# Fourteen projection blocks by seven quarter products, and four pooling gates beside the scan

## Chip, cores, metric

The kernel runs on one core of one Trainium2 chip. The metric is the device time of one execution in microseconds, median of the runs.

## What is computed

One layer of a decoder trunk, all in float32, for x of 1024 tokens by 1024 channels. An RMS norm makes h; one input projection of h (1024 by 13856) is cut into pieces for three branches; each branch is projected back, the three are mixed by sigmoid gates, projected once more, added to x and normed.

```python
h = rms_norm(x, norm_w)
proj = h @ w_in
z, xbc, dt_raw, pool_u, pool_gate, qkv, sb_gate, merge = split(proj)
y_ssm  = mamba2_branch(z, xbc, dt_raw, ...) @ w_proj_ssm    # causal conv of width 4 and SiLU on xbc, then a chunked scan
y_pool = pool_branch(pool_u, pool_gate, ...) @ w_proj_pool  # (trailing means - u) @ pool_w * scale * silu(pool_gate)
y_sb   = stick_breaking_branch(qkv, sb_gate) @ w_proj_sb    # attention with products of (1 - sigmoid), times silu(sb_gate)
g = sigmoid(merge)
merged = g[0] * y_ssm + g[1] * y_pool + g[2] * y_sb
return rms_norm(x + merged @ w_out, final_norm_w)
```

## The kernel before

**Matmuls.** h stands transposed in SBUF, as eight tiles `hT` of 128 channels by 1024 tokens, each as a high part and a low part that together make up the float32 value. The weights are taken in blocks of 256 columns, split in the same way; a product is the three matmuls high-high, high-low, low-high. A block by `gemm_b` is 2 column tiles x 2 token halves x 8 channel tiles x 3 = 96 matmuls of 512 columns (L148). `gemm_a` has the tokens on the other side, 8 token tiles x 24 matmuls of 256 columns (L157), 288 for z0, which takes the 32 dt columns along.

**Weights.** `block_plan` is the list of the 54 input blocks, then those of the output projections. `split_half` takes half a block from a load buffer (two of them): ScalarE casts the high part (L128), VectorE subtracts for the low part (L129), and the next half's load is issued on SP. `block` sees that the halves of its block are split; `mm` hands out PSUM tiles and one split on the way.

**Phases.** First the convolution phase (`conv_part`), where a hand-written order holds for TensorE, VectorE, ScalarE and GpSimd: blocks x0, x1, z0, x2 to x9 (one step of the dt computation, `dt_part`, behind each x block), then g0 to g2, the attention gates. An x block's quarter is read from PSUM by ScalarE (L442) and by three taps on VectorE (L447), then sigmoid (L450), a product on GpSimd (L451) and a store to `d_x`. Three PSUM buffers are added there to the two that all phases share.

Then attention: eight windows, one per pair of heads; in each, matmuls of blocks (v, z, q, k of the next pair, and an `extra` block from `att_fill`) are laid between the attention's own as filling, by a budget in time. Per head and query block: scores (L601, L602), ScalarE (L605, L608), a scan and a product on VectorE (L610, L611), transposes (L628), and the product with v (L651), which waits for VectorE's copy-out `o` (L657). The last window has two filling blocks, m2 and m3.

Then the scan (`ssd_part`) with the eight blocks m4 to m11 as filling, by `merge_gen`, which copies a block to `d_gate`. Then the pool phase (`pool_part`): in turn a u block with the trailing means on VectorE (`mixed`, L728 to L737, up to four adds per column tile for the last group) and a gate block pg with six small matmuls `pp` per quarter (`gated`, L755). Behind it the output projections; their operands x0, x1, ... are loaded from memory and split by `load_x` (L978, L979), the first three of them while the pool phase runs.

## Time and profile before

| | |
|---|---|
| Median of 3 runs | 2082.42 us (2081.85 to 2083.22) |
| Profiled execution | 2080.79 us |
| Its span | 2079.0 us |
| TensorE busy (matmul) | 2048.6 us, 99% |
| VectorE, ScalarE, GpSimd busy | 1203.2, 904.6, 348.9 us |
| Share of the chain that ended last | TensorE 92%, VectorE 4%, ScalarE 2% |

The span is what the profile's rows cover; the profiled execution's own time has 1.8 us around it. A busy time is the sum over an engine's instructions; the chain is the work that ended last, followed back from the end.

### The profile page before, as it was taken

How to read it: one execution, taken by the hardware profiler on the slowest of the kernel's cores; microseconds unless marked ns; L12 is line 12 of the kernel's file. 1: busy time of each engine (PE TensorE's matmuls, PEld its weight loads, DVE VectorE, ACT ScalarE, POOL GpSimd, SP SyncE). 2: the span in 40 equal slices, each digit the busy share in tenths (PEclk: the TensorE clock that was granted, in tenths of full speed). 3: DMA queues.
4: the chain of work that ended last, by engine and by line, in shares of the span. 5: the costliest groups of instructions: out<-in, count | busy, mean ns of one | idle time of the engine just before them, and what ended most of it. 6: DMA issues, size and time to landing. Idle time of an engine off the chain costs nothing.

```text
span 2079.0 us, 29567 instructions
## 1 busy us (share of the span) xinstructions
PE 2048.6 (99%) x11480; PEld 1751.9 (84%) x11480; DVE 1203.2 (58%) x1635; ACT 904.6 (44%) x1841; POOL 348.9 (17%) x415
## 2 busy tenths in 40 slices
PE   8999999999999999999999999999999999999998
PEld 6988889979899998888877877788888888888898
DVE  6466632676666776766774777773545424425333
ACT  5243322555555555555555666763322323323131
POOL 3112200021111111111112344430000002221000
PEclk9999999999999999999999999999999999999999
DMA  4323232112121212212215566654222625433232
GB/s 155 110 94 104 101 104 92 44 54 75 48 72 47 67 57 62 72 41 79 59 51 172 187 203 198 208 163 146 86 76 78 218 96 189 149 101 109 81 133 82
DMA packets 111677, 221.49 MB, mean 107 GB/s; under 512 B 9393, under 2 KB 59313, under 8 KB 111537
## 3 DMA queue, kind: packets, MB, share of 16 engines
q1 hardware_dynamic: 111536, 219.60, 32.4%
q8 instruction: 91, 1.49, 0.3%
q14 instruction: 50, 0.40, 0.1%
HBM read 162.15 MB, written 57.41 MB: 106 GB/s over the span
## 4 chain that ended last, share of the span: by engine, by line
PE 92%; DVE 4%; ACT 2%; issue 1%; DMA 1%; POOL 0%; SPq 0%; DVEq 0%; POOLq 0%; ACTq 0%
PE mm L148 34%; PE mmx L148 24%; PE mm L157 13%; PE mmx L157 4%; PE av L651 3%; PE yd L874 3%; PE tr L628 2%; DVE om L610 2%; PE z L601 1%; PE z L602 1%; PE yo L877 1%; PE st L880 1%; PE pp L755 1%; DVE be L611 1%; PE xp L858 1%
## 5 line engine op out<-in xcount | busy, mean ns | idle before, releaser
L148 PE MATMUL mm<-hT,w 128*128 128x512 f32 x2808 | 717.7, 401 | 3.1 <-DVE hT L345 2.8
L148 PEld LDWEIGHTS mm<-hT,w 128*128 128x128 f32 x2808 | 510.8, 188 | 115.6 <-issue 15.3
L129 DVE TENSOR_TENSOR w<-raw,w 128x1024 fp32r<-128x1024 f32 x142 | 207.7, 1463 | 149.6 <-ACT w L128 149.3
L157 PE MATMUL mm<-w,hT 128*128 128x256 f32 x2112 | 283.9, 286 | 1.2 <-ACT qb L545 1.2
L148 PE MATMUL mmx<-hT,w 128*128 128x512 f32 x1224 | 281.5, 389 | 0.0
L148 PEld LDWEIGHTS mmx<-hT,w 128*128 128x128 f32 x1224 | 229.7, 188 | 47.7
L157 PEld LDWEIGHTS mm<-w,hT 128*128 128x128 f32 x2112 | 263.4, 191 | 2.2 <-ACT qb L545 1.7
L148 PE MATMUL mmx<-x,w 128*128 128x512 f32 x1008 | 230.9, 389 | 0.0
L148 PEld LDWEIGHTS mmx<-x,w 128*128 128x128 f32 x1008 | 189.2, 188 | 39.3
L610 DVE TENSOR_TENSOR_SCAN om<-om,zero 128x128 f32<-128x128 f32 (+7 forms) x128 | 174.4, 1363 | 69.6 <-ACT om L605 69.0
L128 ACT CAST w<-raw 128x1024 fp32r<-128x1024 f32 x142 | 148.6, 1049 | 65.8 <-PE mmx L148 32.3
L630 ACT CAST attT<-tr 128x512 fp32r<-128x512 f32 (+2 forms) x224 | 98.4, 439 | 147.0 <-PE tr L628 79.3
L631 DVE TENSOR_TENSOR attT<-tr,attT 128x512 fp32r<-128x512 f32 (+2 forms) x224 | 111.0, 496 | 76.1 <-ACT attT L630 74.1
L605 ACT ACTIVATE om<-z 128x128 f32<-128x128 f32 (+2 forms) x192 | 92.8, 495 | 78.3 <-PE z L604 75.7
L148 PE MATMUL mm<-x,w 128*128 128x512 f32 x528 | 122.5, 390 | 0.0
L148 PEld LDWEIGHTS mm<-x,w 128*128 128x128 f32 x528 | 98.8, 188 | 21.5 <-ACT x L978 0.7
L1002 ACT ACTIVATE gt<-gt 128x1024 f32<-128x1024 f32 x32 | 34.0, 1062 | 184.0 <-DMA gt<-d_gate 181.3
L851 POOL TENSOR_TENSOR E<-E,cbm 128x1024 f32<-128x1024 f32 x32 | 76.3, 2385 | 161.4 <-issue 121.9
L611 DVE TENSOR_TENSOR be<-be,om 128x128 f32<-128x128 f32 (+7 forms) x128 | 96.9, 757 | 10.4
L1011 POOL TENSOR_TENSOR acc<-acc,gt 128x512 f32<-128x512 f32 x32 | 45.9, 1435 | 293.0 <-DVE gt L1010 293.0
L608 ACT ACTIVATE be<-z 128x128 f32<-128x128 f32 (+2 forms) x192 | 93.0, 498 | 0.1
L628 PE MATMUL tr<-cm,be 128*128 128x128 f32 x576 | 89.5, 273 | 0.5 <-DVE be L611 0.5
(194 smaller groups left out, 2515.6 us busy)
## 6 DMA issues: line engine op xcount, KB each, us to landing
raw<-in_wblk SPq DMA_DIRECT2D x148, 512.0 KB, 3.9
E<-d_act SPq DMA_DIRECT2D x32, 512.0 KB, 4.3
gt<-d_gate SPq DMA_DIRECT2D x32, 512.0 KB, 3.8
d_gate<-mg SPq DMA_DIRECT2D x24, 512.0 KB, 3.4
d_x<-csg SPq DMA_DIRECT2D x16, 512.0 KB, 2.7
xi<-d_x SPq DMA_DIRECT2D x32, 256.0 KB, 3.2
zs<-d_z SPq DMA_DIRECT2D x32, 256.0 KB, 2.8
d_ssm<-yt SPq DMA_DIRECT2D x32, 256.0 KB, 3.1
```

The costliest lines, as they stand in the source:

```text
L128: nc.scalar.copy(hi, raw)
L129: nc.vector.tensor_tensor(out=lo, in0=raw, in1=hi.bitcast(F32), op=ALU.subtract)
L148: T.matmul(ps, w(a, k, ct * P, ct * P + P), mov(b, k, half * 512, half * 512 + 512), start=n == 0, stop=n == 23)
L157: T.matmul(ps, sta(a, k, tok * P, tok * P + P), w(b, k, 0, ncol), start=n == 0, stop=n == 23)
L605: A.activation(om[:, c0 : c0 + n], z[:, 0:n], AF.Sigmoid, scale=-0.125)
L608: A.activation(be[:, c0 : c0 + n], z[:, 0:n], AF.Sigmoid, scale=0.125)
L610: V.tensor_tensor_scan(out=rev, data0=rev, data1=self.zero.broadcast_to((P, L)), initial=1.0, op0=ALU.mult, op1=ALU.add)
L611: V.tensor_tensor(out=be[:, 0:L], in0=be[:, 0:L], in1=om[:, 1 : L + 1], op=ALU.mult)
L628: T.transpose(tr[:, c : c + P], b[:, (2 * jc + j) * P : (2 * jc + j + 1) * P], self.ident)
L630: A.copy(at[:, 0, sl], tr[:, sl])
L631: V.tensor_tensor(out=at[:, 1, sl], in0=tr[:, sl], in1=at[:, 0, sl].bitcast(F32), op=ALU.subtract)
L851: G.tensor_tensor(out=E, in0=E, in1=cbm[:, hg // 2].unsqueeze(1).broadcast_to((P, 8, P)), op=ALU.mult)
```

## The change

Fourteen blocks of the first phase (`SEVEN`: x2 to x9, g2, g3, m4 to m7) are computed by Strassen's scheme in its form with seven products and fifteen sums. A block's weights and h are cut in quarters: weights by channel half and column tile (a11, a12, a21, a22), h by channel half and token half. A product of two quarters is 4 channel tiles x 3 = 12 matmuls of 512 columns.

On h's side four sums of quarters are made once, on VectorE during g0 and g1 (`seven_operands`), split in high and low part by `t_split`, and kept; one of them (t1) takes the place of the upper token half of four hT tiles, which is parked in memory and loaded back behind the last of the blocks (`seven_last`). On the weights' side each block makes four sums (`seven_prep`), in six pieces that stand between the products of the block before. On the output side VectorE makes five adds and ScalarE two copies per block (`seven_block`); six PSUM buffers are added in this stretch. The convolution, gates and stores of a block follow in pieces between the products of the next (`seven_x`, `seven_g`, `seven_m`): an x block now has six taps and two products of 1024 columns on VectorE, and none on GpSimd.

The order in front is now x0, z0, g0, x1, g1 as ordinary blocks. The dt steps stand behind the quarters of x1, where they stood behind whole blocks. Attention's filling has one block less, in the last window only z3. m4 to m7 go to the first phase; the scan's filling is m8 to m11 and the four pg blocks, stored to `d_pg`. In the pool phase `gated` loads the gates from there, in place of a block's matmuls. Smaller: six v buffers for four, two constants made on the chip or loaded later, a smaller DMA scratch.

The diff, cut to its core:

```diff
-    extra = [("g", 3)] + [("z", i) for i in range(1, 4)] + [("m", i) for i in range(4)]
+    extra = [("z", 1), ("m", 0), ("z", 2), ("m", 1), ("m", 2), ("m", 3), ("z", 3)]
...
+SEVEN = [("x", 2), ("m", 4), ("x", 3), ("g", 2), ("x", 4), ("m", 5), ("x", 5), ("m", 6), ("x", 6), ("g", 3), ("x", 7), ("m", 7), ("x", 8), ("x", 9)]
+SCAN_FILL = [(kind, i) for i in range(4) for kind in ("m", "pg")]
+SCAN_FILL = [(kind, i + 8 if kind == "m" else i) for kind, i in SCAN_FILL]
...
-    for i in range(10):
-        part(("x", i), OFF_X + 256 * i)
-        if i == 1:
-            part(("z", 0), OFF_Z + 1024)
-    for i in range(3):
-        part(("g", i), OFF_SG + 256 * i)
+    for kind, i in [("x", 0), ("z", 0), ("g", 0), ("x", 1), ("g", 1)]:
+        part((kind, i), {"x": OFF_X, "g": OFF_SG, "z": OFF_Z + 1024}[kind] + 256 * i)
+    for kind, i in SEVEN:
+        part((kind, i), {"x": OFF_X, "g": OFF_SG, "m": OFF_M}[kind] + 256 * i)
...
-    for i in range(4, 12):
-        merge(i)
-    for g in range(5):
-        if g < 4:
-            part(("u", g), OFF_U + 256 * g)
-        if g > 0:
-            part(("pg", g - 1), OFF_PG + 256 * (g - 1))
+    for kind, i in SCAN_FILL:
+        part((kind, i), {"m": OFF_M, "pg": OFF_PG}[kind] + 256 * i)
+    for g in range(4):
+        part(("u", g), OFF_U + 256 * g)
...
+        def hi(t, c0, c1, src):
+            A.copy(t[:, 0, :, c0:c1], src)
+        def lo(t, c0, c1, src):
+            V.tensor_tensor(out=t[:, 1, :, c0:c1], in0=src, in1=t[:, 0, :, c0:c1].bitcast(F32), op=ALU.subtract)
+        def first():
+            V.tensor_tensor(out=s1, in0=a21, in1=a22, op=ALU.add)
+            V.tensor_tensor(out=s2, in0=s1, in1=a11, op=ALU.subtract)
+        def second():
+            V.tensor_tensor(out=s3, in0=a11, in1=a21, op=ALU.subtract)
+            V.tensor_tensor(out=s4, in0=a12, in1=s2, op=ALU.subtract)
+            hi(t0, 0, P, a11)
+            hi(t2, 0, 256, r1)
+        def third():
+            lo(t0, 0, P, a11)
+            lo(t2, 0, 256, r1)
+            self.load_half()
+            self.load_half()
+        def fourth():
+            hi(t0, P, 256, s2)
+            hi(t1, 0, P, s3)
+        def fifth():
+            lo(t0, P, 256, s2)
+        def sixth():
+            lo(t1, 0, P, s3)
+            hi(t1, P, 256, s1)
+            lo(t1, P, 256, s1)
+            hi(t2, 256, 384, s4)
+            lo(t2, 256, 384, s4)
+        return {1: first, 2: second, 3: third, 4: fourth, 5: fifth, 6: sixth}
...
+        for k in range(4):
+            a, c = self.hT[k], self.hT[4 + k]
+            nc.sync.dma_start(out=self.park[:, k], in_=a[:, :, hi].bitcast(F32))
+            t1 = pool.tile([P, 512], F32, name=f"t1_{k}")
+            d, e = tmp("td"), tmp("te")
+            V.tensor_tensor(out=d, in0=f(a, 0, hi), in1=f(a, 0, lo), op=ALU.subtract)
+            V.tensor_tensor(out=t1, in0=f(a, 1, hi), in1=f(a, 1, lo), op=ALU.subtract)
+            V.tensor_tensor(out=t1, in0=t1, in1=d, op=ALU.add)
+            self.t1.append(t1)
+            V.tensor_tensor(out=e, in0=f(c, 0, hi), in1=t1, op=ALU.subtract)
+            V.tensor_tensor(out=e, in0=e, in1=f(c, 1, hi), op=ALU.add)
+            self.t_split(2, k, e)
+            yield
...
+    def t_split(self, i, k, src):
+        hi, lo = self.tt[i][:, 0, k], self.tt[i][:, 1, k]
+        self.nc.scalar.copy(hi, src)
+        self.nc.vector.tensor_tensor(out=lo, in0=src, in1=hi.bitcast(F32), op=ALU.subtract)
...
+        def product(ps, a, b, first):
+            n = 0
+            for k in range(4):
+                for i, j in ((0, 0), (0, 1), (1, 0)):
+                    T.matmul(ps, w[a](i, k), mov[b](j, k), start=first and n == 0, stop=n == 11, skip_group_check=not first)
+                    n += 1
...
+        x = self.mm()
+        product(x, "a11", "b11", True)
+        A.copy(p1, x)
+        step(0)
+        y = self.mm()
+        product(y, "s2", "t2", True)
+        add(u2, y, p1)
+        step(1)
+        z = self.mm()
+        product(z, "s3", "t3", True)
+        add(u3, z, u2)
+        step(2)
+        v = self.mm()
+        product(v, "s1", "t1", True)
+        add(q(1, 1), v, u3)
+        step(3)
+        product(x, "a12", "b21", False)
+        A.copy(q(0, 0), x)
+        step(4)
+        product(z, "a22", "t4", False)
+        add(q(1, 0), z, u2)
+        step(5)
+        product(v, "s4", "b22", False)
+        add(q(0, 1), v, u2)
+        step(6)
+        return c
...
+        def conv(ct):
+            col = 2 * b + ct
+            nc.gpsimd.memset(c[ct][:, 0:3], 0.0)
+            acc = accs[ct] = self.c_pool.tile([P, S], F32, tag="csg", name="acc", bufs=2)
+            cw = lambda k: self.conv_w[:, col, k : k + 1]
+            nc.scalar.activation(acc, c[ct][:, 3 : 3 + S], AF.Identity, scale=cw(3), bias=self.conv_b[:, col : col + 1])
+            for k in range(3):
+                nc.vector.scalar_tensor_tensor(acc, c[ct][:, k : k + S], cw(k), acc, op0=ALU.mult, op1=ALU.add)
+        def gate(ct):
+            nc.scalar.activation(c[ct][:, 0:S], accs[ct], AF.Sigmoid)
+        def out(ct):
+            col = 2 * b + ct
+            dst = self.d_x[col // 4][:, col % 4] if col < 16 else self.d_bc[:, col - 16]
+            self.silu(c[ct][:, 0:S], accs[ct], c[ct][:, 0:S], dst)
+        return {0: [lambda: conv(0), lambda: gate(0)], 1: [lambda: out(0)], 3: [lambda: conv(1)], 4: [lambda: gate(1)], 5: [lambda: out(1)]}
...
-            nctx = ExitStack()
+            dctx, zctx, nctx = ExitStack(), ExitStack(), ExitStack()
+            dpool = self.sb(dctx, "dt_sb", 1)
+            self.zd = self.sb(zctx, "zd_sb", 1).tile([P, 2, 8, 288], F32R, name="zd")
             norm = self.norm_in(self.sb(nctx, "n_sb", 3), pps)
             for _ in range(3):
                 next(norm)
+            self.drain(self.conv_gen(0, pool, norm))
+            nctx.close()
+            self.zd_open(dpool)
             dt = self.dt_part(dpool)
-            for b in range(10):
-                self.drain(self.conv_gen(b, pool, norm if b == 0 else None))
-                if b == 0:
-                    nctx.close()
-                    self.zd_open(ctx, dpool)
-                else:
+            next(dt)
+            zctx.close()
+            tpool = self.sb(ctx, "t_sb", 1, "right")
+            self.s32pool = self.sb(ctx, "s32_sb", 1, "right")
+            sums = self.seven_operands(tpool)
+            for i, _ in enumerate(self.g_gen(0)):
+                if i % 24 == 12:
+                    next(sums, None)
+            for i, _ in enumerate(self.conv_gen(1, pool)):
+                if i != 3:
                     next(dt, None)
-            for b in range(3):
-                self.drain(self.g_gen(b))
+            self.drain(dt)
+            dctx.close()
+            self.wspool = self.sb(ctx, "ws_sb", 2)
+            self.wseven = {}
+            for i, _ in enumerate(self.g_gen(1)):
+                if i % 18 == 9 and i < 80:
+                    next(sums, None)
+            self.drain(sums)
+            prep = self.seven_prep(BLK[SEVEN[0]])
+            for i in sorted(prep):
+                prep[i]()
+            self.seven_first()
+            plain.close()
+            self.ps_extra(ctx, "seven_ps", 6)
+            make = {"x": self.seven_x, "g": self.seven_g, "m": self.seven_m}
+            before = {}
+            for i, (kind, b) in enumerate(SEVEN):
+                prep = self.seven_prep(BLK[SEVEN[i + 1]]) if i + 1 < len(SEVEN) else {1: self.split_half, 2: self.split_half}
+                before = make[kind](b, self.seven_block((kind, b), before, prep))
+            for i in sorted(before):
+                for f in before[i]:
+                    f()
+            self.seven_last()
...
-                w = self.block(("pg", g))
                 for ct in range(2):
+                    pg = pool.tile([P, S], F32, tag="pgr", name="pgr")
+                    nc.sync.dma_start(out=pg, in_=self.d_pg[:, 2 * g + ct])
                     for half in range(2):
                         hs = slice(half * 512, half * 512 + 512)
-                        ps = self.mm()
-                        self.drain(self.gemm_b(ps, w, ct, self.h, half))
                         sg = pool.tile([P, 512], F32, tag="psg", name="psg")
-                        A.activation(sg, ps, AF.Sigmoid)
-                        V.tensor_tensor(out=sg, in0=sg, in1=ps, op=ALU.mult)
+                        A.activation(sg, pg[:, hs], AF.Sigmoid)
+                        V.tensor_tensor(out=sg, in0=sg, in1=pg[:, hs], op=ALU.mult)
...
-            self.start_fill([(("m", b), self.merge_gen(b)) for b in range(4, 12)])
+            self.start_fill([((kind, b), self.merge_gen(b, kind)) for kind, b in SCAN_FILL])
```

Three places in the order of instructions. First VectorE behind x0's last taps, where the dt columns of z0's weights (`zd`) are made. Before:

```order
L447 SCALAR_TENSOR_TENSOR cacc_343<-mmx_477,cols_158,cacc_343 128x511
L447 SCALAR_TENSOR_TENSOR cacc_343<-mmx_477,cols_158,cacc_343 128x512
L357 CAST zd_514<-wdt_raw_515 128x8x32
L358 TENSOR_TENSOR zd_514<-wdt_raw_515,zd_514 128x8x32
L129 TENSOR_TENSOR zd_514<-raw4_431,zd_514 128x4x256
L430 COPY cacc_523<-cols_158 128x3
L447 SCALAR_TENSOR_TENSOR cacc_523<-mmx_525,cols_158,cacc_523 128x512 x3
L447 SCALAR_TENSOR_TENSOR cacc_523<-mm_554,cols_158,cacc_523 128x510
L447 SCALAR_TENSOR_TENSOR cacc_523<-mm_554,cols_158,cacc_523 128x511
L447 SCALAR_TENSOR_TENSOR cacc_523<-mm_554,cols_158,cacc_523 128x512
```

After:

```order
L681 SCALAR_TENSOR_TENSOR cacc_346<-mmx_478,cols_163,cacc_346 128x511
L681 SCALAR_TENSOR_TENSOR cacc_346<-mmx_478,cols_163,cacc_346 128x512
L591 CAST zd_149<-wdt_raw_514 128x8x32
L592 TENSOR_TENSOR zd_149<-wdt_raw_514,zd_149 128x8x32
L129 TENSOR_TENSOR w4_520<-raw4_433,w4_520 128x1024
L607 TENSOR_TENSOR zsg_550<-zsg_550,mmx_525 128x256
L609 TENSOR_TENSOR dt_x_519<-mmx_525,rows_179 128x32
L607 TENSOR_TENSOR zsg_580<-zsg_580,mm_555 128x256
L609 TENSOR_TENSOR dt_x_519<-mm_555,rows_179 128x32
L129 TENSOR_TENSOR w5_585<-raw5_443,w5_585 128x1024
```

Before, the taps of x1 (`cacc_523`) follow; now z0's own read-outs (`zsg`, `dt_x`) follow, with g0's weights (`w4`) between.

Second, VectorE at the place where the sixth block's weights (`w10`) get their low part. Before, the last dt operations stand ahead of it and x3's taps behind it:

```order
L391 SCALAR_TENSOR_TENSOR dt_all_655<-dt_x_656,dt_ln_1051 128x256
L396 SCALAR_TENSOR_TENSOR adt_1062<-dt_all_655,ea_1060 128x256
L129 TENSOR_TENSOR w10_1064<-raw10_910,w10_1064 128x1024
L430 COPY cacc_1069<-cols_158 128x3
L447 SCALAR_TENSOR_TENSOR cacc_1069<-mm_1071,cols_158,cacc_1069 128x512 x3
L447 SCALAR_TENSOR_TENSOR cacc_1069<-mm_1100,cols_158,cacc_1069 128x510
L447 SCALAR_TENSOR_TENSOR cacc_1069<-mm_1100,cols_158,cacc_1069 128x511
```

After, the sixth block is the first with seven products; `td`, `te` and `tt3` are sums of h's quarters, `gsg` g1's gate products, `s0` to `s3` the block's weight sums, and `w10`, `w11`, `ws5` hold its parts:

```order
L244 TENSOR_TENSOR td_1241<-td_1241,te_1242 128x512
L251 TENSOR_TENSOR tt3_798<-td_1241,tt3_798 128x512
L761 TENSOR_TENSOR gsg_1218<-gsg_1218,mm_1219 128x512
L761 TENSOR_TENSOR gsg_1218<-gsg_1218,mm_1258 128x512
L179 TENSOR_TENSOR s0_1289<-raw10_952,raw11_1040 128x512
L180 TENSOR_TENSOR s1_1290<-s0_1289,raw10_952 128x512
L183 TENSOR_TENSOR s2_1291<-raw10_952 128x512
L184 TENSOR_TENSOR s3_1292<-raw11_1040,s1_1290 128x512
L176 TENSOR_TENSOR w10_1286<-raw10_952,w10_1286 128x4x128
L176 TENSOR_TENSOR ws5_1288<-raw11_1040,ws5_1288 128x4x256
L176 TENSOR_TENSOR w10_1286<-s1_1290,w10_1286 128x4x128
L176 TENSOR_TENSOR w11_1287<-s2_1291,w11_1287 128x4x128
```

What moved there: ahead of the sixth block's weights now stand the sums of h, g1's gate products and that block's weight sums, and the low part is taken in pieces.

Third, TensorE at the end of the pool phase, from the last gate block's end on (`pp` the small matmuls, `x_...` the first operands of the output projections). Before:

```order
L148 MATMUL mm<-hT_109,w_14786 128x512 x3
L755 MATMUL pp<-mx,pw 128x512 x6
L148 MATMUL mm<-x_14538,w_14865 128x512 x3
L148 MATMUL mm<-x_14543,w_14865 128x512 x3
L148 MATMUL mm<-x_14548,w_14865 128x512 x3
L148 MATMUL mm<-x_14538,w_14865 128x512 x3
```

After:

```order
L1020 MATMUL pp<-mx,pw 128x512 x18
L382 MATMUL mm<-x_15023,w_15043 128x512 x3
L1020 MATMUL pp<-mx,pw 128x512 x6
L382 MATMUL mm<-x_15028,w_15043 128x512 x3
L382 MATMUL mm<-x_15033,w_15043 128x512 x3
L382 MATMUL mm<-x_15023,w_15043 128x512 x3
L382 MATMUL mm<-x_15028,w_15043 128x512 x3
L382 MATMUL mm<-x_15033,w_15043 128x512 x3
L382 MATMUL mmx<-x_15023,w_15043 128x512 x3
```

The `pp` rows of the last two groups, which stood apart by 24 matmuls each, now stand together and among the first matmuls on the operands.

## Rows read from the trace of the kernel before

**Rows 1.** The page: busy time by engine, and the chain that ended last.

```profile
PE 2048.6 (99%) x11480; PEld 1751.9 (84%) x11480; DVE 1203.2 (58%) x1635; ACT 904.6 (44%) x1841; POOL 348.9 (17%) x415
...
PE 92%; DVE 4%; ACT 2%; issue 1%; DMA 1%; POOL 0%; SPq 0%; DVEq 0%; POOLq 0%; ACTq 0%
```

**Rows 2.** The chain in order of time (start us, us, what), first phase.

```profile
53.59 10.88 PE mm L148 x48
64.47 5.44 PE mmx L148 x24
...
336.10 23.03 PE mm L157 x192
```

**Rows 3.** TensorE's waits over the run: releaser, us in total, times, longest.

```profile
PE av L651 <- DVE o L657: 9.5, 10, 1.7
```

**Rows 4.** Timeline, end of x0 (start us, us, what, [idle before <-releaser]).

```profile
49.02 2.32 DVE L447 SCALAR_TENSOR_TENSOR cacc<-mmx,cols,cacc 128x510 f32<-128x510 f32 x3 [3.13 <-ACT cacc L442]
...
51.25 0.28 DVE L357 CAST zd<-wdt_raw 128x256 fp32r<-128x256 f32 x1
...
51.57 0.42 DVE L358 TENSOR_TENSOR zd<-wdt_raw,zd 128x256 fp32r<-128x256 f32 x1
```

**Rows 5.** Timeline, the first and last dt step during block x3.

```profile
121.54 0.40 ACT L378 ACTIVATE dt_ab<-dt_x 128x256 f32<-128x256 f32 x1
...
128.67 0.43 DVE L396 SCALAR_TENSOR_TENSOR adt<-dt_all,ea 128x256 f32<-128x256 f32 x1
```

**Rows 6.** Groups by form: count | busy us, mean ns | idle before.

```profile
L129 DVE TENSOR_TENSOR w<-raw,w 128x1024 fp32r<-128x1024 f32 x142 | 207.7, 1463 | 149.6 <-ACT w L128 149.3
...
L450 ACT ACTIVATE csg<-cacc 128x1024 f32<-128x1024 f32 x20 | 21.2, 1062 | 47.1 <-DVE cacc L447 29.7 <-DVE cacc L430 17.4
...
L781 ACT COPY mg<-mm 128x512 f32<-128x512 f32 x48 | 28.0, 584 | 38.4 <-PE mm L148 38.2
...
L447 DVE SCALAR_TENSOR_TENSOR cacc<-mm,cols,cacc 128x512 f32<-128x512 f32 x36 | 27.0, 750 | 5.0 <-ACT cacc L442 3.7
...
L1011 DVE TENSOR_TENSOR acc<-acc,gt 128x512 f32<-128x512 f32 x16 | 11.1, 692 | 0.5
...
L734 DVE SCALAR_TENSOR_TENSOR u<-s,u 128x1024 f32<-128x1024 f32 x8 | 9.8, 1226 | 0.3
```

**Rows 7.** Window of a head pair late in attention (columns in the first line).

```profile
core 0: us, PE busy (x) PEld busy (x) DVE busy (x) ACT busy (x) POOL busy (x), PEclk, DMA share, GB/s
1032.70:1068.60 35.90, 33.55 (x191) 27.40 (x190) 27.41 (x37) 20.40 (x47) 5.62 (x15) 1.00 0.19 59
```

**Rows 8.** Timeline, a pooled-mean chain, and TensorE and ScalarE at the pool phase's end.

```profile
1565.21 1.24 DVE L728 TENSOR_TENSOR s<-u 128x1039 f32<-128x1039 f32 x1 [9.29 <-ACT u L722]
...
1573.32 1.23 DVE L737 TENSOR_TENSOR mx<-u,mx 128x1024 fp32r<-128x1024 f32 x1 [1.17 <-ACT mx L736]
...
1628.24 1.52 PE L755 MATMUL pp<-mx,pw 128*128 128x512 f32 x6
...
1636.86 1.05 ACT L978 CAST x<-xraw 128x1024 fp32r<-128x1024 f32 x1 [6.88 <-DMA xraw<-d_sb]
```

**Rows 9.** Windows round two of TensorE's pauses (PEclk is the granted clock).

```profile
548.00:550.00 2.00, 1.29 (x8) 1.09 (x8) 1.60 (x3) 1.63 (x5) 0.84 (x1) 0.86 0.42 109
550.00:552.00 2.00, 2.00 (x12) 2.00 (x11) 1.72 (x3) 1.31 (x2) 0.44 (x1) 0.50 0.63 200
552.00:554.00 2.00, 2.00 (x16) 1.96 (x16) 1.10 (x2) 0.71 (x3) 0.00 (x0) 0.78 0.72 173
1128.00:1130.00 2.00, 2.00 (x12) 1.65 (x11) 1.68 (x3) 1.98 (x6) 0.00 (x0) 1.00 1.06 386
```

**Rows 10.** Timeline, the pauses themselves.

```profile
547.75 0.61 PE L157 MATMUL mm<-w,hT 128*128 128x256 f32 x3 [1.23 <-ACT qb L545]
549.08 0.93 PE L651 MATMUL av<-attT,vb 128*128 128x256 f32 x4 [0.71 <-DVE o L657]
...
1127.62 0.66 PE L858 MATMUL xp<-cm,xi 128*128 128x128 f32 x4 [2.45 <-DMA xi<-d_x]
```

More of the change, by code (lines that the diff above doesn't have):

```diff
@@ L112, in split_half @@
         n = self.wnext
[L113 removed]
+        if n >= self.limit():
             return
@@ new lines, in t_split, with seven_first @@
+    def t_split(self, i, k, src):
+        hi, lo = self.tt[i][:, 0, k], self.tt[i][:, 1, k]
+        self.nc.scalar.copy(hi, src)
+        self.nc.vector.tensor_tensor(out=lo, in0=src, in1=hi.bitcast(F32), op=ALU.subtract)
+    def seven_first(self):
+        nc = self.nc
+        for k in range(4):
+            hi, lo = (self.hT[k][:, i, 512:1024] for i in range(2))
+            nc.scalar.copy(hi, self.t1[k])
+            nc.vector.tensor_tensor(out=lo, in0=self.t1[k], in1=hi.bitcast(F32), op=ALU.subtract)
@@ new lines, in seven_g, with gate, out, seven_m @@
+    def seven_g(self, b, c):
+        nc = self.nc
+        sgs = {}
+        def gate(ct):
+            sgs[ct] = self.c_pool.tile([P, S], F32, tag="csg", name="gsg", bufs=2)
+            nc.scalar.activation(sgs[ct], c[ct][:, 3 : 3 + S], AF.Sigmoid)
+        def out(ct):
+            self.silu(sgs[ct], c[ct][:, 3 : 3 + S], sgs[ct], self.d_g[:, 2 * b + ct])
+        return {0: [lambda: gate(0)], 1: [lambda: out(0)], 2: [lambda: gate(1)], 3: [lambda: out(1)]}
+    def seven_m(self, b, c):
+        def part(ct):
+            col = 2 * b + ct
+            self.nc.sync.dma_start(out=self.d_gate[col // 8][:, col % 8], in_=c[ct][:, 3 : 3 + S])
+        return {0: [lambda: part(0), lambda: part(1)]}
@@ L448, in conv_gen @@
             if half == 1:
-                sg = pool.tile([P, S], F32, tag="csg", name="csg")
+                sg = pool.tile([P, S], F32, tag="csg", name="csg", bufs=2)
                 nc.scalar.activation(sg, acc[:, 0:S], AF.Sigmoid)
@@ L703, in pool_part @@
             ppw = self.ps(ctx, "p_pw", 2)
+            self.inv = pool.tile([P, 4, 16], F32, name="inv", bufs=1)
+            nc.sync.dma_start(out=self.inv, in_=self.ins["inv"])
             parts = {}
```

119 lines of the change are left out of this document (99 added, 20 removed).

## The prediction

> **What bounds the kernel now.** I read the page first: busy time by engine and the chain that ended last [rows 1]. TensorE is busy 99% of the span and makes up 92% of the chain, so a matmul that goes is time that goes, as long as TensorE then waits for nothing new. Next the chain in order of time in the first phase [rows 2]: a run of 48 matmuls of 512 columns takes 10.88 us, so one takes 226.7 ns, a block of 96 takes 21.76 us, and a quarter of a block 5.44 us. Third, TensorE's waits: the one that recurs is attention's, for VectorE's `o` [rows 3]. Hence the question for each part: does VectorE (58% busy) or ScalarE (44%) come late somewhere when TensorE has less to do in front of them?
>
> **The change, part by part.** All sums are made against the profiled execution: span 2079.0 us, 2080.8 us with what lies around it. The median of the runs is 2082.4 us, 1.6 us more; I add the net to the median.
>
> *What goes.* A block done by seven products has 7 x 12 = 84 matmuls where 96 stood. Fourteen blocks: 168 x 0.2267 = **38.1 us saved**, if they run at the old rate. A block becomes 84 x 0.2267 = 19.04 us. The number of blocks stays 54; the four gate blocks and the m blocks only change places, at equal price.
>
> *z0 directly behind x0.* z0's 32 dt columns are made on VectorE behind x0's last taps: taps until 51.34 us, then 0.28 and 0.42, ready at 51.99 [rows 4]. Before, x1 lay between. x1 ended when z0 began, at 69.91 us [rows 2]; 21.76 us earlier, at 48.15, x0 ended. So TensorE waits 51.99 - 48.15 = **3.8 us** (3.4 to 4.1).
>
> *dt steps a quarter block apart.* The chain from the first ScalarE step to `adt` took 129.10 - 121.54 = 7.6 us, mostly table loads and the reciprocal [rows 5]; a whole block hid it. Now the chain starts a quarter into x1 (5.44 us, plus one evacuation of 0.78) and the next step's matmul stands at 10.88 us in TensorE's row. It gets its input at 5.44 + 0.8 + 7.6 = 13.8 us or a little later: 3.2 us of wait. The step after that waits for a copy that stands behind a tap group on VectorE (three of 0.75 us [rows 6]): 0 to 2.3, I take 1.4. Together **4.6 us** (3 to 6).
>
> *Start of the seven-product blocks.* During g1, VectorE gets 26 sums of 128x512 and g1's four gate products: 30 x 0.692 = 20.8 us [rows 6] (the `acc` row, same shape and type). Six of the sums' results go to ScalarE for a cast (0.58 us [rows 6], 0.75 with both handovers), and VectorE's next instruction needs that cast: 6 x 0.75 = 4.5. x1's last evacuation and taps come first: 0.78 + 3 x 0.75 = 3.0, with handover 3.2. Then four weight sums and the first low part, 5 x 0.692 = 3.5, before the first product may start. Total 32.0 us against TensorE's 21.76: **10.2 us of idle TensorE** (7.5 to 12). What hides nothing here: after g1 there is no other matmul in TensorE's row.
>
> *Inside the phase.* Per block VectorE has 14 operations of 128x512 (4 weight sums, 5 low parts, 5 result adds) and one of 128x1024: 14 x 0.692 + 1.23 = 10.9 us. In the block after an x block come the convolution's six taps and two products at 128x1024, 8 x 1.23 = 9.8 us [rows 6] (the 1226 ns row). 20.7 us against 19.04: VectorE ends 1.66 us late, and the next block's first two products need low parts that stand at the end of its row. This happens after six of the pairs (before x3, x4, x5, x6, x7, x8): 6 x 1.66 = **10.0 us**. Ends: 3 us if each operation is 6% shorter than its row, since an operation followed at once by the next starts it a little before its own end; 22 us if they take as long as the weight subtract's mean of 1463 ns instead of 1226 [rows 6]. I take the rows of the same shapes.
>
> *Leaving the phase.* Behind x9's last product VectorE still has an add, six taps, two products and the casts and sigmoids of ScalarE between them: 0.69 + 1.06 + 3.7 + 1.06 + 1.23 + 3.7 + 1.06 + 1.23 = 13.7, with a weight split (1.23) and handovers 16.3 us. vz0's tiles take 23.03 / 4 = 5.76 us [rows 2] and have two PSUM buffers; the third may start when the first is read out, at 16.3 + 2.1 = 18.4, instead of at 11.5: **6.9 us** (5 to 11).
>
> *Attention's last window.* Two blocks (43.5 us) filled it, now one z block (23.0 us). A head pair took 35.90 us with TensorE busy 33.55 and VectorE 27.40 [rows 7]: 2.35 us of waits. 20.5 us less over 2.3 such pairs leaves TensorE 24.6 per pair and VectorE about 26 (the block's weight splits go with it). VectorE and the chain of a head now decide; with a pair at 29.3 us the waits are 4.7, 2.4 more than before: 2.3 x 2.4 = **5.5 us** (0, if the waits stay, to 10, if a pair takes 31 us).
>
> *End of the pool phase.* x3's load stands on SP behind the last store of the pool gates; its cast came 6.88 us after ScalarE's last work, and x3 was ready at 1637.91, 8.15 us after the last pp matmul at 1629.76 [rows 8]. Before, 36 matmuls on x0 to x2 (8.2 us) filled just that. Now the last pp has 20 of them behind it, 4.5 us: 3.6 us of wait. u3's mean chain (9.34 us for a column tile [rows 8]) has 5.4 us of pp and 4.8 us of matmuls as cover, so hardly a wait: 0.4. **4.0 us** (2.8 to 6). The gate loads that are new lie on SP long before their use.
>
> *The clock.* Two pauses, 1.23 and 0.71 us, brought the granted clock to 0.86, 0.50 and 0.78 in three stretches of 2 us [rows 9, 10]: (0.14 + 0.50 + 0.22) x 2 = 1.7 us lost. A single pause of 2.45 us left it at 1.00 in the next stretch. I count the two longest new pauses (start and exit): **3.4 us** (0 to 9, five falls).
>
> Losses: 3.8 + 4.6 + 10.2 + 10.0 + 6.9 + 5.5 + 4.0 + 3.4 = 48.4. Net 48.4 - 38.1 = +10.3 us: **2082.4 + 10.3 = 2093 us** (the profiled execution 2091).
>
> **The rivals.**
>
> *VectorE is never late in the phase (faster).* Its place is the stretch from g1 to vz0, its price the three terms that hang on VectorE: 10.2 + 10.0 + 6.9 = 27.1 us, which gives 2093 - 27 = 2066. It starts to decide at 8% shorter operations, where the 20.7 us fit into 19.04 and the 10 us inside the phase are gone (with 2 to 3 us at the start, 2080). The start goes only if a sum takes (21.76 - 3.2 - 4.5 - 3.5) / 30 = 0.35 us, or if the casts' round trips vanish too. For it: the taps' rows include the wait for the previous result, independent sums may overlap. Against it: the 692 ns row had only 0.5 us of idle time in front of 16, so that is the pace in a row. The middle of this case is about even (2079 to 2086), its far end 2062.
>
> *VectorE is slower than in its quiet rows (slower still).* If the operations take what the weight subtract takes in the mean, 19% more, 12 us come inside the phase, 5 at the start, 4 at the exit: 2114. For it: the new DMA traffic and ScalarE's doubled casts there. Against it: GpSimd, which shared that stretch before, has only memsets now.
>
> *The clock falls at every pair.* Six times a pair of pauses, 0.65 and 1.0 us, like the pair at 546 us. At 1.7 us each that is 10 us, so 2103. For it [rows 9, 10]; against it, a head pair with 2.35 us of waits kept a clock of 1.00 [rows 7]. The Trainium skill, "TensorE: Matmul & The Clock Gate", section "A second HAM failure mode: psum-queue depth-cycling", says that short idle spells of TensorE between groups of matmuls, when frequent, make the clock swing between its two levels; by that, this rival would be the forecast, and the sum 2103. The two pauses at 546 us agree with it, the pause before 1128 us doesn't speak on it.
>
> *The change doesn't give its 168 matmuls.* Products of 12 in place of runs of 24 could each lose a hand-over of 0.2 us at their PSUM buffer: 98 x 0.2 = 20 us, 2113. Against it: tiles of x 24 follow each other at 226.7 ns [rows 2], six buffers are to be had.
>
> **How the numbers follow.** Forecast with its own spread (2087 to 2099): 0.42. VectorE less late, about even (2079 to 2087): 0.18; fully in time (2062 to 2078): 0.17. Slower VectorE 0.11, clock at every pair 0.09, matmuls not gained 0.03. 0.2% or 4 us is about what a measurement of this kernel can tell from no change, so the bounds are 2078.3 and 2086.6: faster 0.17, about the same 0.18, slower 0.65. The terms' lower ends all at once would give 2069, their upper ends 2124; a range that leaves out about one in ten on either side is **2070 to 2109**.
>
> **What would show it.** In the profile after: TensorE's busy time about 38 us lower (2010); idle TensorE of 4 us before z0, 3 and 1.4 us at the dt steps in x1, 10 us before the first product with VectorE busy all through g1, pauses for `w` before six x blocks, some 7 us before vz0's third tile, 4 us around the first use of x3. Wrong would be: VectorE idle before the first product, no pauses at the x blocks, or a run of 84 matmuls that takes over 19.5 us without a wait.

## The result, and the profile after

The changed kernel takes 2111.99 us (median of 4 runs, 2109.11 to 2115.31) against 2082.22 us of the kernel before (4 runs beside it): 1.0143 times as long, 95% interval 1.0125 to 1.016. 168 matmuls are gone and the kernel is 30 us slower. Forecast was 10 us slower, 2093 us, with a range of 2070 to 2109: the right sign, a third of the size, and a time outside the range.

The changed kernel's page, busy time by engine and chain [rows 1]:

```profile
PE 2035.8 (96%) x11312; PEld 1733.3 (82%) x11312; DVE 1327.7 (63%) x1821; ACT 947.4 (45%) x1921; POOL 311.6 (15%) x416
...
PE 77%; DVE 14%; ACT 4%; issue 3%; DMA 2%; SPq 0%; POOL 0%; DVEq 0%; ACTq 0%; POOLq 0%
```

TensorE's busy time fell by 12.8 us, not by 38.1: matmuls at a lower clock and at a slower pace, 16.6 and 6.5 us in the table below, are most of the difference. Its idle time rose by 44.7 us. VectorE went from 4% to 14% of the chain. TensorE's waits in the changed kernel (releaser: us in total, times, longest), beside the single row of [rows 3]:

```profile
PE av L915 <- DVE o L921: 13.5, 10, 3.7
PE mm L391 <- issue: 9.7, 1, 9.7
PE mm L285 <- ACT w L173: 7.1, 1, 7.1
PE mm L382 <- ACT x L1244: 5.6, 1, 5.6
PE mmx L634 <- DVE adt L630: 3.8, 1, 3.8
PE mmx L391 <- DVE zd L591: 3.4, 1, 3.4
PE sm L1104 <- DMA bcin<-d_bc: 3.3, 1, 3.3
...
PE mm L285 <- DVE w L176: 2.3, 1, 2.3
```

In this order: attention, most of it the last window; vz0's third tile, which needs the PSUM buffer of the first (`issue` stands where the profile shows no releaser); the first product of the first seven-product block; x3 in the output projections; the dt step; z0; the scan's start; the first product once more, in its low part. Before, only the first of these waits was above 0.2 us.

Behind each of these places, and of the ten waits for `o` behind the two longest (2.3 and 3.7 us), TensorE ran at its lower clock (0.50) for some microseconds. Windows of 2 us of the changed kernel (span, then busy us of PE, PEld, DVE, ACT, POOL, then the granted clock), at z0, the dt step, the first product, vz0, the last window twice, the scan's start and the pool phase's end:

```profile
54.00:56.00 2.00, 2.00 (x11) 2.00 (x10) 2.00 (x1) 0.00 (x0) 1.21 (x2) 0.50 0.06 23
118.00:120.00 2.00, 2.00 (x6) 1.55 (x5) 1.20 (x2) 0.66 (x1) 0.00 (x0) 0.50 0.00 0
164.00:166.00 2.00, 1.44 (x3) 1.16 (x4) 2.00 (x3) 2.00 (x5) 0.00 (x0) 0.50 0.22 70
462.00:464.00 2.00, 1.88 (x9) 1.92 (x10) 0.35 (x2) 0.00 (x0) 0.00 (x0) 0.50 0.92 278
1168.00:1170.00 2.00, 2.00 (x10) 2.00 (x10) 1.35 (x3) 0.27 (x1) 1.87 (x2) 0.50 0.00 0
1182.00:1184.00 2.00, 2.00 (x11) 1.91 (x11) 0.72 (x2) 1.00 (x3) 0.10 (x1) 0.50 0.46 86
1236.00:1238.00 2.00, 2.00 (x7) 1.61 (x6) 1.73 (x3) 1.97 (x4) 0.00 (x0) 0.50 1.03 394
1674.00:1676.00 2.00, 2.00 (x6) 1.59 (x5) 1.95 (x3) 2.00 (x3) 0.00 (x0) 0.50 0.76 242
```

The kernel before had one such fall between its start and its end [rows 9], this one eight. Busy time times (1 - granted clock), summed over all windows of 2 us, is what the low clock costs: 3.9 us before, 20.5 us after.

The span of the profiled execution grew by 31.9 us. What makes it up, from the waits, the clock windows and the starts of the products:

| Step | forecast, us | waits measured, us | low clock behind it, us |
|---|---|---|---|
| matmuls that go | -38.1 | -38.1 | |
| z0 behind x0 | 3.8 | 3.4 | 3.2 |
| dt steps | 4.6 | 4.0 | 2.9 |
| start of the seven-product blocks | 10.2 | 9.4 | 2.0 |
| inside the phase | 10.0 | 6.5 | 0 |
| leaving it (1.8 + 9.7) | 6.9 | 11.5 | 2.8 |
| attention's last window, scan's start | 5.5 | 9.1 | 5.5 |
| end of the pool phase | 4.0 | 6.7 | 2.0 |
| clock | 3.4 | | (sum 18.4; whole run 20.5 less the 3.9 of before: 16.6) |

The 6.5 us inside the phase are no idle time but a slower pace. The losses come to 50.6 + 16.6 = 67.2, less 38.1 is 29.1; 2.8 us of the span's growth are in none of the rows.

### The profile page after: what moved, and what is told of

It reads as the page before. It is cut to its first block, busy times and chain, and to the rows that moved or that the text cites. A ratio compares the mean times of both kernels' runs of the same rounds, so it can differ in the third digit from the quotient of the medians.

```text
span 2110.9 us, 29563 instructions
## 1 busy us (share of the span) xinstructions
PE 2035.8 (96%) x11312; PEld 1733.3 (82%) x11312; DVE 1327.7 (63%) x1821; ACT 947.4 (45%) x1921; POOL 311.6 (15%) x416
## 4 chain that ended last, share of the span: by engine, by line
PE 77%; DVE 14%; ACT 4%; issue 3%; DMA 2%; SPq 0%; POOL 0%; DVEq 0%; ACTq 0%; POOLq 0%
PE mm L382 25%; PE mmx L382 13%; PE mm L391 13%; PE mmx L285 5%; PE mmx L391 4%; PE av L915 3%; PE yd L1140 3%; DVE om L874 2%; DVE acc L344 2%; PE tr L892 2%; PE mm L285 2%; PE z L865 1%; PE yo L1143 1%; PE z L866 1%; PE st L1146 1%
## 5 line engine op out<-in xcount | busy, mean ns | idle before, releaser
L382 PE MATMUL mm<-hT,w 128*128 128x512 f32 x2232 | 581.1, 405 | 5.0 <-DVE hT L578 3.1
L382 PEld LDWEIGHTS mm<-hT,w 128*128 128x128 f32 x2232 | 408.3, 190 | 98.3 <-issue 15.3
L391 PE MATMUL mm<-w,hT 128*128 128x256 f32 x2112 | 293.9, 288 | 9.7 <-issue 9.7
L391 PEld LDWEIGHTS mm<-w,hT 128*128 128x128 f32 x2112 | 268.3, 192 | 10.8 <-issue 9.9
L129 DVE TENSOR_TENSOR w<-raw,w 128x1024 fp32r<-128x1024 f32 x116 | 157.2, 1355 | 106.1 <-ACT w L128 105.6
L128 ACT CAST w<-raw 128x1024 fp32r<-128x1024 f32 x116 | 121.5, 1051 | 54.6 <-PE mmx L382 24.4
L382 PE MATMUL mmx<-hT,w 128*128 128x512 f32 x456 | 104.9, 390 | 0.0
L382 PEld LDWEIGHTS mmx<-hT,w 128*128 128x128 f32 x456 | 85.4, 188 | 17.6
```

Of the source, the lines that this page charges most:

```text
L128: nc.scalar.copy(hi, raw)
L129: nc.vector.tensor_tensor(out=lo, in0=raw, in1=hi.bitcast(F32), op=ALU.subtract)
L382: T.matmul(ps, w(a, k, ct * P, ct * P + P), mov(b, k, half * 512, half * 512 + 512), start=n == 0, stop=n == 23)
L391: T.matmul(ps, sta(a, k, tok * P, tok * P + P), w(b, k, 0, ncol), start=n == 0, stop=n == 23)
```

## Experiments

Each ratio is to the kernel before, run beside it on the same chip; the changed kernel stands at 1.0143, which is 30 us. A difference between two versions has the intervals of both in it, some 5 us either way for the single edits, so a smaller one shows nothing.

**Keep the clock.** Matmuls without use in four of the stalls, here at z0 and at vz0:

```diff
+            self.idle(14, pps, "tp")
...
+            if p == 0 and t2 == 2:
+                self.idle(42, self.pz, "z")
```

> Theory: behind each long stall TensorE runs at the lower clock for some 4 to 6 us, and that is 11 of the 32 us (3.2 at z0, 2.9 at the dt steps, 2.0 at the first product, 2.8 at vz0, by the granted clock in the rows of the changed kernel). Matmuls whose result nobody reads, put into these four stalls and no longer than they are (14, 16, 40 and 42 of 227 ns), leave the waits as long as they are and keep the clock: 2101 us, granted clock 1.00 behind the four places. Rival: the waits alone cost, the clock follows them without a price of its own: 2112 us.

Measured 2103.83 us, 1.0110 (1.0095 to 1.0125): 7 us less than the changed kernel. One wait is new, 2.0 us at the last dt step. Windows of this run behind the restarts at z0 (51.4 us), at the dt step (114.2) and at vz0 (456.7), columns as above:

```profile
52.00:54.00 2.00, 2.00 (x15) 2.00 (x16) 0.71 (x1) 1.26 (x2) 1.60 (x1) 1.00 0.39 156
116.00:118.00 2.00, 2.00 (x10) 1.62 (x10) 0.32 (x1) 1.57 (x2) 0.00 (x0) 1.00 0.00 0
...
456.00:458.00 2.00, 1.83 (x14) 1.44 (x13) 0.75 (x2) 0.42 (x2) 0.00 (x0) 1.00 0.92 303
```

The clock is 1.00 where it was 0.50, and the time follows. So the low clock has a price of its own behind a stall. By the windows it was 2.0 to 3.2 us at each of these four places, 11 us; the gain of 7 is smaller, the new wait takes 2 of the rest, and the intervals allow the other 2.

**The order alone.** Fourteen ordinary blocks in the changed kernel's order, no sums:

```diff
+            make = {"x": lambda b: self.conv_gen(b, pool), "g": self.g_gen, "m": self.merge_gen}
+            for kind, b in SEVEN:
+                self.drain(make[kind](b))
```

> The changed kernel's order of blocks, with pooling gates beside the scan, but the fourteen blocks are ordinary ones of 96 matmuls, without sums and parked halves. Theory: of the 70 us that eat up the 38 saved, z0 (6.6 with its low clock), the dt steps (6.9), attention's last window (12) and the end from the scan on (11) come from the order alone; start, inside and exit of the phase (32) from the seven products: 2080 + 37 = 2117 us. Rival: the order costs nothing by itself, only beside VectorE's sums: 2090 us or less.

Measured 2115.77 us, 1.0169 (1.0155 to 1.0183): 35 us slower than before without a single product saved. TensorE's waits there:

```profile
PE av L891 <- DVE o L897: 13.7, 10, 3.8
PE mm L379 <- ACT x L1220: 5.1, 1, 5.1
PE sm L1080 <- DMA bcin<-d_bc: 3.4, 1, 3.4
PE mmx L388 <- DVE zd L588: 3.4, 1, 3.4
PE mmx L631 <- DVE adt L627: 2.9, 1, 2.9
```

The same rows as in the changed kernel without the three of the phase itself. Of the 37 us by which this run's span is longer than before, 24 are idle TensorE and 11 low clock. More than half of what ate up the gain has nothing to do with Strassen's scheme: it is blocks taken away from where they covered something. The seven products bring 38 us, lose some 32 at the start, inside and at the end of their phase, and are worth the 5 us by which the changed kernel beats this one, a difference hardly larger than its interval.

**The starts.** z0's dt columns before x0's last taps, dt steps in g0 and further apart, two pieces of the sums from g1 into x1, the first block's weight sums ahead of g1's last gate products:

```diff
+            for i, _ in enumerate(self.conv_gen(0, pool, norm)):
+                if i == 2:
+                    self.zd_open(dpool)
...
+                if i == 16:
+                    next(dt)
...
+                if i % 2 == 0:
+                    next(dt, None)
+                else:
+                    next(sums, None)
```

> z0's dt columns are made before x0's last taps, the softplus step of dt stands in g0, the two others behind x1's first and third quarter, and of the sums of h two pieces move from g1 into x1, so that the first block's weight sums stand in the middle of g1. Theory: all three stalls come from where these steps stand in VectorE's row: 3.4 + 4.0 + 9.4 us of waits and 8 us of low clock go, 2088 us (2086 to 2094). Rival: VectorE has too much work from x0 to g1 wherever it stands: the wait comes back before the first product, or in x1 and g1, 2103 us or more.

Measured 2108.07 us, 1.0126 (1.0111 to 1.0141). The waits of z0 and dt are gone, and one has grown; TensorE's waits:

```profile
PE mm L285 <- DVE gsg L767: 16.1, 1, 16.1
```

3.4 + 4.0 + 9.4 = 16.8 us were waited before in three places, 16.1 now in one, and the 3.5 us of gain are within the interval. From z0's end to the first product (74.0 to 158.1 us) VectorE is busy for 69.0 of 84.1 us, and for 8.3 more it stands still for ScalarE's casts of the sums:

```profile
DVE tt L251 <- ACT tt L250: 8.3, 12, 0.7
```

So the rival is right in the main: VectorE has little free time there, and the stalls say where its surplus shows. Some of the 16.1 us are the edit's own: 3.5 us of low parts that only later products need (153.85 to 157.40) stand ahead of the gate products that the first product waits for.

**Less work on VectorE.** On top of the starts' edits, four of 13 sums per channel tile on GpSimd, low parts a sum later, the first block's weight sums later in g1:

```diff
-            V.tensor_tensor(out=d, in0=f(a, 0, hi), in1=f(a, 0, lo), op=ALU.subtract)
+            G.tensor_tensor(out=d, in0=f(a, 0, hi), in1=f(a, 0, lo), op=ALU.subtract)
```

> As a2_starts, but four of the 13 sums of h per channel tile go to GpSimd, the low parts are taken one sum later, so that VectorE doesn't stand still for ScalarE's casts (12 x 0.69 us in a2_starts), and the first block's weight sums stand behind g1's third gate product. Theory: in a2_starts VectorE had no free time from z0's end to the first product, and the wait of 16.1 us was its surplus of work; here it has 16 x 0.69 + 12 x 0.69 = 19 us less, the wait falls under 4 us and the low clock behind it goes: about 20 us less than a2_starts, 2088 us. Rival: GpSimd's sums (1.4 us each, 16 of them) slow VectorE's down or come late themselves: a wait of 8 us or more stays, 2098 us or more.

Measured 2107.17 us, 1.0130 (1.0115 to 1.0145): no gain beyond the interval. Timelines of VectorE and of GpSimd in g0, and of GpSimd alone in x1:

```profile
78.71 1.67 DVE L240 TENSOR_TENSOR te<-hT,t 128x512 f32<-128x512 f32 x1
80.41 0.69 DVE L241 TENSOR_TENSOR te<-te,hT 128x512 f32<-128x512 f32 x1
...
78.09 1.73 POOL L237 TENSOR_TENSOR te<-hT,hT 128x512 f32<-128x512 f32 x1
...
123.12 1.29 POOL L233 TENSOR_TENSOR td<-hT 128x512 f32<-128x512 f32 x1
```

A sum on VectorE takes 0.69 us alone and 1.67 us beside one on GpSimd, one on GpSimd 1.29 and 1.73: the two engines hold each other up. Between z0's end and the first product VectorE is busy for 61.8 us, 7 us less than before this edit, though sums worth 11 us left its row: the rest came back as longer rows. And in place of ScalarE's casts it now waits for GpSimd's sums:

```profile
DVE t L238 <- POOL t L234: 8.6, 2, 7.4
```

TensorE's wait before the first product falls from 16.1 to 12.5 us (10.7 and 1.9), and 4.3 us are new in x1 and g1.

**End on m7.** The phase ends on a block without a convolution:

```diff
-("x", 7), ("m", 7), ("x", 8), ("x", 9)]
+("x", 7), ("x", 8), ("x", 9), ("m", 7)]
```

> The last seven-product block is m7 in place of x9, the rest as it was, so that x7, x8, x9 follow each other. Theory: x9's convolution on VectorE holds up vz0's read-out: 1.8 + 9.7 us of waits and 2.8 us of low clock go, against 2 to 4 us that VectorE's excess costs in three x blocks in a row: 2101 us. Rival: it is the parked halves of hT and the stores ahead of them on SP that come late: a wait of over 5 us stays between m7 and vz0's end, 2107 us or more.

Measured 2103.91 us, 1.0107 (1.0092 to 1.0122): 7 us less. vz0's wait for its buffer falls from 9.7 to 1.1 us, and no low clock follows:

```profile
454.53 11.75 PE L391 MATMUL mm<-w,hT 128*128 128x256 f32 x96 [1.14 <-issue]
```

The tail of x9 on VectorE was the cause of that wait.

**The last window.** First moving a block into it from window 6:

```diff
-    for p in range(1, 7):
+    for p in range(1, 6):
```

> Attention's window 6 gives its third block (m3) to the last window, which then has two as in the kernel before. Theory: waits of the last window fall from 12.7 to about 5 us, the wait of 3.3 us at the scan's start and three falls of the clock (5.5 us) go, window 6 gets waits of about 5: 2101 us. Rival: VectorE and ScalarE are the bound of a window with two blocks too, the waits only move to window 6: 2108 us or more.

Measured 2109.26 us, 1.0135 (1.0118 to 1.0151): the rival. Waits for `o` are 15.4 us in 13 places instead of 13.5 in 10, the longest (3.5 us) now in window 6; a window with two blocks waits, whichever it is:

```profile
PE av L915 <- DVE o L921: 15.4, 13, 3.5
```

Then giving attention its block back, m7, as an ordinary one:

```diff
+    extra = [("z", 1), ("m", 0), ("z", 2), ("m", 1), ("m", 2), ("m", 3), ("z", 3), ("m", 7)]
```

> m7 is an ordinary block again and fills attention's last window beside z3; thirteen blocks keep seven products. Theory: the missing block in attention costs some 8 us of waits there, 3.3 us at the scan's start and 4 us of low clock, and 2.7 us of matmuls come back: 12 us less than the changed kernel, 19 us over the kernel before. Rival: as moving a block from window 6 did nothing, the waits are set by the attention itself: within 4 us of the changed kernel.

Measured 2102.64 us, 1.0105 (1.0090 to 1.0120): 8 us less. TensorE's waits for `o`:

```profile
PE av L915 <- DVE o L921: 8.4, 9, 1.7
```

The 13.5 us fall below the 9.5 of before [rows 3], and the scan's start no longer waits for `bcin`. It is the missing block, not its place. That the gain is 8 us and not the 12 expected goes with the end of the pool phase, where the waits are 2.7 us longer in this run (x3 6.9 us, pp 2.5).

**A gate block back.** pg3 in the pool phase, m7 in its place beside the scan:

```diff
+SCAN_FILL[-1] = ("m", 7)
...
+    part(("pg", 3), OFF_PG + 256 * 3)
```

> The last gate block (pg3) is computed in the pool phase again, behind u3, and m7 fills its place beside the scan; thirteen blocks keep seven products. Theory: the gate block covers the way from the last pp matmul's result to x3's load and split: the wait of 5.6 us, a further us and 2 us of low clock go, 2.7 us of matmuls come back: 6 us less than the changed kernel, 24 us over the kernel before. Rival: x3 waits for hT's buffers and the loads on SP, wherever the gate block stands: a wait of 4 us or more stays, no gain.

Measured 2104.57 us, 1.0118 (1.0103 to 1.0133): 5 us less, hardly more than the interval; x3's wait is 1.5 us instead of 5.6, and no low clock follows it:

```profile
PE mm L384 <- ACT x L1254: 1.5, 1, 1.5
```

**All together**, with twelve blocks by seven products:

```diff
+SEVEN = [("x", 2), ("x", 3), ("g", 2), ("x", 4), ("x", 5), ("m", 4), ("x", 6), ("x", 7), ("g", 3), ("x", 8), ("x", 9), ("m", 5)]
```

> All edits at once: starts and sums as in b1, pg3 in the pool phase, m6 in attention's last window and m7 beside the scan as ordinary blocks, twelve blocks by seven products, in an order that ends on m5. 144 matmuls fewer than before, 32.6 us. Theory: with the stalls gone there remain 5.6 us inside the phase and a few us of waits at its ends: 2080.7 - 32.6 + 5.6 + 8 = 2062 us (2056 to 2070). Rival: what is taken from the stalls comes back elsewhere, since VectorE's work per matmul has grown: 2076 us or more.

Measured 2082.93 us, 1.0015 (1.0005 to 1.0024): the changed kernel's 30 us are gone but for 3, and the time is 21 us over the forecast. VectorE's surplus at the start is still there, a wait of 9.1 us before the first product and 6 us around it. Without GpSimd:

```diff
-            G.tensor_tensor(out=d, in0=f(a, 0, hi), in1=f(a, 0, lo), op=ALU.subtract)
+            V.tensor_tensor(out=d, in0=f(a, 0, hi), in1=f(a, 0, lo), op=ALU.subtract)
...
+        if early:
+            hi(t0, 0, P, a11)
+            lo(t0, 0, P, a11)
```

> As b4_together, but all sums of h on VectorE again, still with the low parts one sum later, and the first block's first low part ahead of its weight sums. Twelve blocks by seven products. Theory: in b4_together GpSimd's sums stretched VectorE's beside them (1.66 to 3.49 us where one alone takes 0.69) and were waited for; without them the wait of 9.1 us before the first product falls to about 3, the 2.7 and 1.6 us in x1 and g1 to 1: 10 us less than b4_together, 2072 us. Rival: VectorE's own work, 11 us more than in b4_together, costs as much as the contention did: 2080 us or more.

Measured 2078.11 us, 0.9991 (0.9982 to 1.0): 5 us less than with GpSimd, half of what was expected, and hardly faster than the kernel before. Before the first products TensorE still waits 10.9 us in two places:

```profile
PE mm L299 <- DVE gsg L781: 10.9, 2, 8.2
```

With GpSimd's sums it was 15.3 us in four places (9.1, 2.7, 1.9, 1.6). So GpSimd's help cost more than it gave, and VectorE's surplus stays. With one more ordinary block as cover:

```diff
+    for kind, i in [("x", 0), ("z", 0), ("g", 0), ("x", 1), ("g", 1), ("g", 2)]:
```

> As c1_twelve, but g2 is an ordinary block too and stands behind g1, in front of the eleven blocks by seven products. Theory: 21.8 us of ordinary matmuls cover VectorE's sums fully; no wait and no fall of the clock before the first product, for 2.7 us more of matmuls: as c1_twelve or 2 to 3 us less, 2070 us. Rival: c1_twelve has no wait left there: 2.7 us more than c1_twelve.

Measured 2072.12 us, 0.9962 (0.9948 to 0.9976): 8 us faster than before, 6 us less than with twelve blocks, and the fastest version here. The wait before the first product is gone; 6.4 us are left in g2, for its second weight half:

```profile
PE mmx L396 <- ACT w L130: 6.4, 1, 6.4
```

The last run was to put that split ahead of the last piece of the sums:

```diff
+                    while self.wnext < 2 * BLK["g", 2] + 2:
+                        self.split_half()
```

> As c2_eleven, but g2's second weight half is split before the last sums of h and not behind them. Theory: the wait of 6.4 us in g2 and 2 us of low clock behind it go: 8 us less, 2064 us. Rival: VectorE is full there, and what g2 doesn't wait for, the first product does: within 3 us of c2_eleven.

Measured 2072.76 us, 0.9960 (0.9946 to 0.9973): no gain, and the wait is still 6.4 us. The edit changes nothing: `block` has split both halves of g2 before the loop's first step, the added loop finds nothing left to split, and the two programs have the same instructions in the same order. So this run repeats the one before, and neither its theory nor its rival was tried. In both, the cast of that weight half stands in ScalarE's row behind the casts of sums begun in g1; an edit that pulls it ahead of those wasn't tried.

## Why the prediction was wrong

**The clock** is the step that failed most: 16.6 us instead of 3.4, 13 of the 22 us by which the span's growth of 31.9 us exceeds the forecast's 10.3. Two things in it were wrong. The count: only the two longest new stalls were given a fall, because one pause of 2.45 us had left the clock at 1.00 [rows 9, 10]. Stalls of 3.4 and 3.8 us lay above anything that the trace of before showed in its middle, and I sided with the nearest row below them. All of them pulled the clock down, and so did two pauses of 2.3 and 3.7 us in attention's last window. The price: 1.7 us came from the one fall that the trace had, which followed two short pauses; behind the eight stalls of the changed kernel it was 1.5 to 3.2 us. The upper bound of 9 us was five times the 1.7, and held neither the count nor the price. "Keep the clock" shows the price, 7 us of it for four places.

**Leaving the phase**, 6.9 us, was 11.5. VectorE's tail from the last add on took 14.2 us (446.1 to 460.3), close to the 13.7 of the sum; but that add ended 5.4 us after the last product, because VectorE had stood still before. VectorE and TensorE there:

```profile
437.13 0.69 DVE L295 TENSOR_TENSOR cx<-mmx,cx 128x512 f32<-128x512 f32 x1 [3.79 <-DMA d_bc<-cx]
...
445.45 0.68 DVE L295 TENSOR_TENSOR cx<-mmx,pu 128x512 f32<-128x512 f32 x1
...
459.10 1.22 DVE L329 TENSOR_TENSOR cx<-cx,acc 128x1024 f32<-128x1024 f32 x1 [1.26 <-ACT cx L347]
460.24 0.48 DVE L777 TENSOR_TENSOR va<-mm,va 128x128 fp32r<-128x128 f32 x2
...
462.12 14.23 PE L391 MATMUL mm<-w,hT 128*128 128x256 f32 x96 [9.70 <-issue]
```

An add waits 3.8 us for the store of the block before to leave its buffer. The reloads of hT are issued on the same queue just around that store (428.6 and 433.8 us, the store 430.5). That they are what delays it is likely, but no run took them away; the sum counted VectorE's and ScalarE's instructions and not the buffers that stores hold.

**Attention's last window**, 5.5 us, was 9.1, of which 3.1 is the scan's first load, which the window's filling had hidden; I had costed only the wait that recurs. **The end of the pool phase**, 4.0 us, was 6.7: the matmuls behind the last pp took 4.7 us, near the 4.5 of the sum, but x3 was ready 10.1 us after it (1662.0 to 1672.1) and not 8.15. ScalarE's last sigmoid waits for a store to leave its `psg` buffer, and the last pp's result waits for that gate:

```profile
1662.84 0.63 ACT L1014 ACTIVATE psg<-pgr 128x512 f32<-128x512 f32 x1 [1.26 <-DMA d_pool<-psg]
```

So x3's load left SP 3.5 us after the last pp (1665.5), where it was 2.4 before, and it took 1 us longer to reach the cast.

**Inside the phase**, 10.0 us, was 6.5, and not for the reason given. TensorE, four products around the start of a block behind an m block:

```profile
204.27 2.88 PE L285 MATMUL mm<-hT,w 128*128 128x512 f32 x12
206.99 3.32 PE L285 MATMUL mm<-tt,w 128*128 128x512 f32 x12
210.16 2.96 PE L285 MATMUL mmx<-tt,w 128*128 128x512 f32 x12
212.96 2.92 PE L285 MATMUL mmx<-hT,w 128*128 128x512 f32 x12
```

The second product takes 3.17 us from start to start, 0.4 over its neighbours: that is all VectorE is late for a pair, not 1.66, and 2.2 us for the six. The rest is a slower pace of the products on the sums of h. VectorE in the same stretch:

```profile
195.94 0.69 DVE L179 TENSOR_TENSOR s<-raw,raw 128x512 f32<-128x512 f32 x1
...
206.98 0.68 DVE L176 TENSOR_TENSOR w<-s,w 128x512 fp32r<-128x512 f32 x1
207.58 0.68 DVE L295 TENSOR_TENSOR cx<-mmx,pu 128x512 f32<-128x512 f32 x1
...
209.38 0.68 DVE L176 TENSOR_TENSOR ws<-s,ws 128x512 fp32r<-128x512 f32 x1
```

From 195.94 to 210.06 us it waits for nothing and does 13 operations of 128x512 and 5 of 128x1024 in 14.1 us; by the durations that the sum took from the rows they are 15.1. The duration of an operation is not the pace in a row: the two in the middle, neither of which needs the other, start 0.60 us apart, and each takes 0.68. The prediction named this case (6% shorter, 3 us) and took the durations. So the rival in which VectorE is in time held for this stretch, nearly, and failed at its two ends, where it was to hold as well: it was three questions put as one. Of the signs of being wrong, the missing pauses at the x blocks came, but for 0.4 us; a run of 84 matmuls without a wait took 19.36 us (184.91 to 204.27), under the 19.5.

That two other rivals had 2114 and 2113 us is chance: VectorE's operations were not longer, and a block's products lose 0.3 us, not 1.4. The sum of the first was also too small: 19% on all of a pair's 20.7 us is 24 us for six pairs; 12 holds for the operations of 1024 columns alone.

**Right** were z0 (3.8 us forecast, 3.4 measured), the dt steps (4.6 and 4.0) and the start (10.2 and 9.4), each from counting what stands in VectorE's row ahead of the instruction that TensorE needs. At the dt steps the sum came nearer than its parts: 3.8 and 0.2 us for 3.2 and 1.4. The starts' run adds what the forecast did not see: these three are in the main one surplus. The rival in which the clock falls at every pair, with the Trainium skill's "A second HAM failure mode: psum-queue depth-cycling" ("TensorE: Matmul & The Clock Gate") behind it, did not come; but its pauses didn't either, 0.4 us for a pair in place of 0.65 and 1.0, so this run can't decide on it. One of the windows of 10 us of the phase, with such a pause in it:

```profile
200.00:210.00 10.00, 9.91 (x44) 7.76 (x43) 9.93 (x12) 4.35 (x7) 0.00 (x0) 1.00 0.44 147
```

The granted clock is 1.00 in this and in all others from 170 to 430 us. What did happen is what the same page has in "HAM oscillation — how this bites in real kernels", that a TensorE left waiting between bursts starts the next one at half rate; the rows above agree, at eight places.

The order of the errors says more than their sizes. The forecast had 17.9 us for what the new order costs (z0, the dt steps, the last window, the pool phase's end), and no fall of the clock at any of these places. The order alone costs 35 us: a block is also cover, and the five places that lost theirs had none to spare.

## What to carry to other kernels

When work is moved or taken from the engine that sets the time, list for each place it leaves what that work was hiding, and cost that first; here it was nearly as large as the whole saving. A new stall of the matmul engine of some microseconds is to be costed with the slow restart that can follow it, 1.5 to 3.2 us each in the changed kernel. And before spreading new vector work over a stretch, sum the stretch: if VectorE has hardly any free time from one end to the other, moving its steps mostly moves the wait.
